# A two-block transformer kernel on one core: 176 stores of what GpSimd has written change from SyncE's queue to GpSimd's

## The chip, the cores and the metric

The kernel runs on one core of a Trainium2 chip. The metric is the time of one execution on the device, in microseconds (us), measured three times for the kernel before. Engine names are those of the profile: PE (TensorE), DVE (VectorE), ACT (ScalarE), POOL (GpSimd), SP (SyncE, which here only issues DMAs). PEclk is the clock that TensorE was granted, as a share of full speed.

## What is computed

A sequence of 2048 tokens of width 1024 goes through two blocks in float32. The first block (window attention, an HGRN2 branch, a mixture of experts) is not touched and is left out here. The second block, cut to what matters:

```python
xn = rms_norm(h, norm_gain)
qa, ka, va, ga, qb, kb, vb, gb, iq, ik, iw, za, zb = split(xn @ w_in)
ya = chunked_relpos_attention(qa, ka, va, rel_bias) * silu(ga)
qb, kb = partial_rope(qb, 16), partial_rope(kb, 16)
iq, ik = partial_rope(iq, 8), partial_rope(ik, 8)
yb = dsa_sparse_attention(qb, kb, vb, iq, ik, iw) * silu(gb)
merged = sigmoid(za + b0) * (ya @ w_branch_a) + sigmoid(zb + b1) * (yb @ w_branch_b)
h = rms_norm(h + merged @ w_out, final_norm_gain)
```

Both attentions have 8 heads of 64. The chunked one sees a band of 9 chunks of 64 keys; the sparse one picks up to 256 keys for each query by the score that iq, ik and iw give.

## The kernel before, in words

**Who sets the order.** The kernel carries a planner of its own. Each piece of work is a generator (a lane) that yields until the planner's clock says that its operands and its engine are free (`b.on(engine, tiles)`), and then emits its instruction. The order in which the generators are let through is the order of the instructions on each engine, and every engine, SP's DMA queue among them, works through its own in that order. `Engine.__getattr__` (from L100) wraps every call, so nearly all instructions have line L111; `Engine.cost` (from L123) gives the planner each call's cost. A `dma_start` there costs its bytes on a shared DMA time and nearly nothing on the issuing engine; an `indirect_dma_start` (GpSimd's gathers) costs 1.04 on GpSimd.

**The second block** is class S3 (from L1846). Its run (L2784) goes through stages, in the profile at about these times:

- to 2026 us: the norm (`norm_lane`), into which the end of the first block is woven (the combine step gathers two expert rows per token block with GpSimd's indirect DMAs, tiles `cy`, and adds them to `cx`), and the projections of the first half of the sequence that are needed by rows: `rows` (16 token blocks in all, 8 per half) makes a 128x256 piece of the projection on PE, `ev_n` (L2047) evicts it through ACT into a ring of three `st` tiles, has GpSimd rotate it in place (`rotate`, six small operations on `rot` and `st`), and stores it to DRAM through `store` (L2037): `IQ` (g = 1, one per token block) and `QB` (g = 2 and 3, two per token block), 128 KB each.
- 2026 to 2337 us: `chunked(0)`, the chunked attention of the first half in 32 units, with other projections on PE between them (the fill). `a_loads` (L2174) loads for every two units `K` (two DMAs), `Q` (four) and `V`, two buffers each, and for every eight units the bias `rb` (one buffer). `a_unit` makes scores on PE (`pS<-K,Q`), adds the bias and takes the maximum on DVE, exponentials on ACT; GpSimd normalises (`sc<-sc,ast`), PE transposes (`pT<-ident,sc`), ACT and DVE split the result into two parts (`pp`), and PE multiplies by V (`pU<-pp,V`). GpSimd copies part of the result (`ot<-up`), and `gate` (L2339) multiplies `ot` by the gate `sg` on GpSimd and stores it to `YT`, 64 KB, through `store`. `gate_load` (L2333) loads `sg` into two buffers.
- 2337 to 2985 us: the rest of the fill, then `sparse` over blocks 0 to 9, with the second half's row projections as fill. It ends every unit with the same `gate`. The normalised input of the second half is loaded from `XND` into `xnh` and `xnl` at the start, and `IQ` and `QB` are read back in tiles `x`.
- 2985 to 3340 us: `chunked(1)`, as chunked(0), for the second half; then the rest of its fill to about 3404 us.
- to the end: `sparse` over blocks 10 to 15, with the output part `tail` as fill. It loads gated rows from `YT` into `yt` (eight loads, one per chunk of the sequence) and gate values from `TZ`, adds with GpSimd (`m<-tz`) and multiplies with the output weights.

**The stores in question.** `store` waits until the planner sees the tile ready for "sync", issues the DMA on SP, and marks the tile done. 16 `IQ`, 32 `QB` and 128 `YT` stores are executed. What SP has behind a store, loads of K, Q, V, weights (`whi`, `wlo`) and gates, comes after it in SP's order.

Of the kernel before, what the change touches and what calls it, by code (L numbers as in the profile page):

```python
# [10 lines left out]
F32 = mybir.dt.float32  # L11
# [81 lines left out]
class Engine:  # L93
# [11 lines left out]
    def __getattr__(self, f):  # L105
        real = getattr(self.eng, f)
        if not callable(real) or f in ("preload_act_table_set",):
            return real

        def call(*a, **k):  # L110
            r = real(*a, **k)  # L111
            out = k.get("out", a[0] if a else None)
            if is_ap(out):
                outs = [out] + [k[x] for x in ("accum_out",) if is_ap(k.get(x))]
                ins = [x for x in a[0 if "out" in k else 1:] if is_ap(x)]
                ins += [x for y, x in k.items() if y not in ("out", "accum_out") and is_ap(x)]
                ins += [x.ap for x in k.values() if hasattr(x, "ap") and not is_ap(x) and is_ap(x.ap)]
                cost, lat = self.cost(f, out, ins, k, [x for x in a + tuple(k.values()) if isinstance(x, AF)])
                self.clock.op(self.name, outs, ins, cost, lat, 1.46 if f == "indirect_dma_start" else 0.0)
            return r  # L120
        return call

    def cost(self, f, out, ins, k, fs):  # L123
        n = out.free_size()
        if f in ("dma_start", "indirect_dma_start"):
            b = out.size() * 4 if callable(out.size) else out.size * 4
            return (1.04, 0.0) if f != "dma_start" else (b / 3.6e5, 0.0)
        if self.name == "tensor":
            if f == "transpose":
                return 0.109, 0.1  # L130
            if ins[0].dtype == F32:
                return max(0.2, n * 0.0017), 0.1
            return max(0.107, n * 0.000423), 0.1
        ps = any(x.space == PSUM for x in ins) or out.space == PSUM
        m = max([n] + [x.free_size() for x in ins])
        if self.name == "vector":
            if f in ("tensor_scalar", "tensor_copy", "memset") and not ps and "accum_out" not in k:
                return 0.067 + n * 0.00055, 0.07
            if f == "reciprocal":
                return 0.06 + n * 0.0063, 0.07  # L140
            return 0.067 + (0.05 if "accum_out" in k else 0.0) + m * 0.00107, 0.07
        if self.name == "scalar":
            aps = is_ap(k.get("scale")) + is_ap(k.get("bias")) + ("accum_out" in k)
            return self.switch(next((x for x in fs if hasattr(x, "name")), None)) + (0.052 if ps else 0.1) + m * 0.00083 + 0.09 * aps, 0.1
        return 0.13 + n * (0.00088 if f == "tensor_scalar" else 0.00217), 0.1
# [50 lines left out]
class B:  # L196
# [101 lines left out]
    def store(self, dst, t, tile=None):  # L298

        yield from self.do("sync", "dma_start", dst, t)  # L300
        self.done(t if tile is None else tile)
# [1544 lines left out]
class S3:  # L1846
# [187 lines left out]
                yield from b.on("tensor")  # L2034
        b.spawn(self.ev_n(g, blk, ps))

    def store(self, dst, t, src=None, key=None):  # L2037

        b = self.b
        yield from b.on("sync", t)  # L2040
        self.nc.sync.dma_start(dst, t.bitcast(F32) if src is None else src)
        b.done(t)
        if key:
            self.flags.add(key)
        yield 1

    def ev_n(self, g, blk, ps):  # L2047
# [14 lines left out]
        elif g:  # L2062
            h = 8 if g == 1 else 4
            x = yield from self.stage([128, h, 256 // h])
            yield from b.on("scalar", ps, x)
            nc.scalar.activation(x, ps[:, 0:256].rearrange("p (h d) -> p h d", h=h), AF.Copy)
            b.done(ps)
            yield 1
            yield from b.on("gpsimd", x)
            if g == 1:  # L2070
                self.rotate(x, rp[:, 16:20], rp[:, 20:24], 8, 4)
                dst, key = self.IQ[r, :], ("iq", blk)
            else:
                self.rotate(x, rp[:, 0:8], rp[:, 8:16], 4, 8)
                dst, key = self.QB[r, (g - 2) * 256:(g - 2) * 256 + 256], ("qb", blk, g - 2)
            yield 1
            yield from self.store(dst, x, x.rearrange("p h d -> p (h d)"), key)
        else:
            x = yield from self.stage([128, 424])
            yield from b.on("scalar", ps, x)  # L2080
            nc.scalar.activation(x[:, 0:160], ps[:, 0:160], AF.Copy)
            nc.scalar.activation(self.iw[:, blk], ps[:, 160:168], AF.Copy, scale=1.0 / 16)
            b.done(ps)
            nc.scalar.activation(self.vbS[:, blk, 0], x[:, 64:128], AF.Copy)
            yield 1
            yield from b.on("vector", x)
            b.lo(self.vbS[:, blk, 1], x[:, 64:128], self.vbS[:, blk, 0])
            yield 1
            yield from b.on("gpsimd", x)
            self.rotate(x[:, 0:64].unsqueeze(1), rp[:, 0:8], rp[:, 8:16], 1, 8)  # L2090
            self.rotate(x[:, 128:160].unsqueeze(1), rp[:, 16:20], rp[:, 20:24], 1, 4)
            xx = x[:, 168:424].rearrange("p (i d) -> p i d", i=2)
            nc.gpsimd.tensor_copy(xx[:, 0].rearrange("p (a d) -> p a d", a=2), x[:, 0:64].unsqueeze(1).to_broadcast([128, 2, 64]))
            nc.gpsimd.tensor_copy(xx[:, 1].rearrange("p (a d) -> p a d", a=4), x[:, 128:160].unsqueeze(1).to_broadcast([128, 4, 32]))
            yield 1
            pt = yield from b.bank("pT")
            yield from b.on("tensor", xx, pt)
            for i in range(2):
                nc.tensor.transpose(pt[:, i * 128:i * 128 + 128], xx[:, i], b.ident)
            b.done(x)  # L2100
            yield 1
            kk, ii = self.kbS[:, r], self.ikS[:, r]
            yield from b.on("scalar", pt)
            nc.scalar.activation(kk, pt[:, 0:128], AF.Copy)
            nc.scalar.activation(ii, pt[:, 128:256], AF.Copy)
            yield 1
            yield from b.on("vector", kk)
            b.lo(kk[64:128], pt[64:128, 0:128], kk[64:128])
            b.lo(ii[32:64], pt[32:64, 128:256], ii[32:64])
            b.lo(ii[96:128], pt[96:128, 128:256], ii[96:128])  # L2110
            b.done(pt)
            self.flags.add(("kb", blk))
            yield 1
# [225 lines left out]
    def gate(self, ot, g, i, blk):  # L2339

        b = self.b
        yield from b.G("tensor_tensor", ot, ot, g, op=OP.mult)
        b.done(g)
        yield from self.store(self.YT[i, :, blk * 128:blk * 128 + 128], ot, None, ("y", i, blk))

    def a_units(self, half):
        for p in range(4):
# [690 lines left out]
```

## Time and profile before

| | |
|---|---|
| runs | 4229.81, 4234.5 and 4241.1 us, median 4234.5 |
| the profiled execution | 4238.96 us, of it 4237.1 us in the profile's span |
| PE busy | 3719.6 us, 88% of the span |
| DVE busy | 2733.3 us, 65% |
| ACT busy | 2263.5 us, 53% |
| POOL busy | 787.0 us, 19% |
| mean granted clock | 0.939 |

Matmuls overlap, so the busy time of PE is the time in which at least one is under way. A wait is put down to what came last by the profile; "SPq" is SP's DMA queue, and a wait of SPq means that its next DMA had not been issued yet. DMAs that SP issues are shown with the time that the issue took on SP.

### The profile page before, as it was taken

What the parts mean: (1) busy time and instruction counts of PE and PEld (TensorE: products, weight loads), DVE (VectorE), ACT (ScalarE), POOL (GpSimd) and SP (SyncE); (2) the same over time, 40 slices, a digit from 0 to 9 for tenths busy, and PEclk for the clock granted to TensorE, in tenths of its full rate; (3) what the DMA queues carried; (4) which work ended last, traced back from release to release, by engine and by line L of the source; (5) the groups of instructions that cost most, each with busy time, mean ns of one, the idle gap of its engine ahead of it and who ended that gap; (6) DMA issues with size and microseconds to landing.
All of it is one profiled execution on the core that took longest, in us unless ns stands there. A gap on an engine that the chain in (4) does not pass through costs nothing. (4 is left out here: it accounts for less than half of the span.)

```text
span 4237.1 us, 64813 instructions
## 1 busy us (share of the span) xinstructions
PE 3719.6 (88%) x21649; PEld 3211.7 (76%) x21649; DVE 2733.3 (65%) x7027; ACT 2263.5 (53%) x4628; POOL 787.0 (19%) x1474
## 2 busy tenths in 40 slices
PE   3999999979889995779888899998788979998895
PEld 2888788768768884778777798886677868997685
DVE  7866875787777776562445256777544248878772
ACT  3644645556456664342334167886444238876851
POOL 1310000131011112650334242000222101111000
PEclk9999999979999997899989989999899999999898
DMA  6232542144288886588888834432666488886154
GB/s 221 80 130 73 183 141 90 34 144 140 105 303 316 310 312 248 196 314 275 272 240 265 293 111 133 142 111 63 177 176 189 135 270 299 298 282 222 48 183 172
DMA packets 451953, 815.32 MB, mean 192 GB/s; under 512 B 129712, under 2 KB 269968, under 8 KB 450704
## 3 DMA queue, kind: packets, MB, share of 16 engines
q1 hardware_dynamic: 440080, 777.42, 55.2%
q0 software_dynamic: 11520, 33.57, 2.5%
q8 instruction: 176, 2.88, 0.3%
q14 instruction: 177, 1.45, 0.1%
HBM read 589.56 MB, written 229.65 MB: 193 GB/s over the span
## 5 line engine op out<-in xcount | busy, mean ns | idle before, releaser
L111 PE MATMUL pA<-xnl,whi 128*128 128x512 f32 x1024 | 417.8, 408 | 2.9 <-POOL whi L111 2.9
L111 DVE TENSOR_TENSOR wlo<-ld,whi 128x1024 fp32r<-128x1024 f32 x271 | 325.1, 1230 | 140.4 <-POOL whi L111 74.0
L111 ACT ACTIVATE pp<-pT 128x256 fp32r<-128x256 f32 (+1 forms) x568 | 260.8, 478 | 283.7 <-PE pT L111 277.4
L111 PE MATMUL pA<-xnh,wlo 128*128 128x512 f32 x1024 | 407.1, 398 | 2.3 <-DVE wlo L111 2.3
L111 PE MATMUL pA<-xnh,whi 128*128 128x512 f32 x1024 | 407.5, 398 | 0.0
L111 DVE TENSOR_TENSOR pp<-pT,pp 128x256 fp32r<-128x256 f32 (+1 forms) x568 | 295.9, 539 | 138.7 <-ACT pp L111 135.6
L111 PE MATMUL pA<-hlo,whi 128*128 128x512 f32 x832 | 352.8, 424 | 10.0 <-issue 6.6
L111 PE MATMUL pA<-hhi,wlo 128*128 128x512 f32 x832 | 329.7, 396 | 0.0
L111 PE MATMUL pA<-hhi,whi 128*128 128x512 f32 x832 | 328.9, 395 | 0.0
L111 PE MATMUL pU<-pp,vbS 128*128 128x256 f32 x1088 | 217.2, 311 | 34.5 <-DVE pp L111 23.3
L111 ACT ACTIVATE whi<-ld 128x1024 fp32r<-128x1024 f32 x212 | 213.3, 1052 | 50.7 <-PE pA L111 35.0
L111 DVE SCALAR_TENSOR_TENSOR acc<-rl,iw,acc 128x512 f32<-128x512 f32 (+3 forms) x304 | 212.7, 700 | 36.2 <-ACT rl L111 26.4
L111 PEld LDWEIGHTS pA<-xnh,wlo 128*128 128x128 f32 x1024 | 196.3, 192 | 47.3 <-DVE wlo L111 3.4
L111 PE MATMUL pA<-wlo,xnh 128*128 128x256 f32 (+1 forms) x672 | 205.0, 305 | 24.4 <-ACT st L111 5.9
L111 ACT ACTIVATE bias<-acc,sst 128x384 f32<-128x384 f32 (+13 forms) x168 | 219.9, 1309 | 8.6 <-DVE sst L111 6.1
L111 PEld LDWEIGHTS pA<-xnl,whi 128*128 128x128 f32 x1024 | 197.3, 193 | 33.6 <-POOL whi L111 3.3
L111 PEld LDWEIGHTS pA<-xnh,whi 128*128 128x128 f32 x1024 | 197.3, 193 | 30.2
L111 PEld LDWEIGHTS pU<-pp,vbS 128*128 128x128 f32 x1088 | 164.0, 198 | 53.6 <-DVE pp L111 33.5
L111 PE MATMUL pA<-whi,xnl 128*128 128x256 f32 (+1 forms) x672 | 200.0, 298 | 4.1 <-DMA xnl<-XND 4.1
L111 PE MATMUL pA<-whi,xnh 128*128 128x256 f32 (+1 forms) x672 | 199.8, 297 | 0.0
L111 PE MATMUL pS<-kbS,qd 128*128 128x512 f32 (+3 forms) x640 | 186.4, 391 | 13.5 <-DVE bst L111 9.6
L111 PE MATMUL pS<-K,Q 128*128 128x320 f32 (+3 forms) x480 | 117.7, 354 | 79.8 <-DMA Q<-QA 75.7
(491 smaller groups left out, 10993.7 us busy)
## 6 DMA issues: line engine op xcount, KB each, us to landing
whi<-W2P SPq DMA_DIRECT2D x172, 512.0 KB
wlo<-W2P SPq DMA_DIRECT2D x172, 512.0 KB
ld<-in_w_gu_dram SPq DMA_DIRECT2D x128, 512.0 KB
ld<-in_w_dn_dram SPq DMA_DIRECT2D x64, 512.0 KB
W2P<-whi SPq DMA_DIRECT2D x57, 512.0 KB
W2P<-wlo SPq DMA_DIRECT2D x57, 512.0 KB
Y<-ym SPq DMA_DIRECT2D x48, 512.0 KB
K<-KA SPq DMA_DIRECT2D x48, 384.0 KB
```

Source lines behind the costliest of these rows:

```text
L111: r = real(*a, **k)
```

## The change

`store` gets an argument for the engine that issues the DMA. The rotated queries (`IQ`, `QB`) and the gated rows (`YT`) are issued on GpSimd's queue, all other stores stay on SP's. The planner prices a plain DMA of an engine other than SP as it prices a gather: 1.04 on the engine, and its bytes on the DMA time.

```diff
-                self.clock.op(self.name, outs, ins, cost, lat, 1.46 if f == "indirect_dma_start" else 0.0)
+                far = 1.46 if f == "indirect_dma_start" else out.size() * 4 / 3.6e5 if f == "dma_start" and self.name != "sync" else 0.0
+                self.clock.op(self.name, outs, ins, cost, lat, far)
...
-            return (1.04, 0.0) if f != "dma_start" else (b / 3.6e5, 0.0)
+            return (1.04, 0.0) if f != "dma_start" or self.name != "sync" else (b / 3.6e5, 0.0)
...
-    def store(self, dst, t, src=None, key=None):
+    def store(self, dst, t, src=None, key=None, eng="sync"):
 
         b = self.b
-        yield from b.on("sync", t)
-        self.nc.sync.dma_start(dst, t.bitcast(F32) if src is None else src)
+        yield from b.on(eng, t)
+        getattr(self.nc, eng).dma_start(dst, t.bitcast(F32) if src is None else src)
...
-            yield from self.store(dst, x, x.rearrange("p h d -> p (h d)"), key)
+            yield from self.store(dst, x, x.rearrange("p h d -> p (h d)"), key, "gpsimd")
...
-        yield from self.store(self.YT[i, :, blk * 128:blk * 128 + 128], ot, None, ("y", i, blk))
+        yield from self.store(self.YT[i, :, blk * 128:blk * 128 + 128], ot, None, ("y", i, blk), "gpsimd")
```

On SP, at the end of sparse blocks 0 to 9 and the start of chunked(1) (numbers behind the names are buffers), the order before:

```order
L111 DMA YT<-ot_32974 128x128
L111 DMA sg_33060<-SG 128x128
L111 DMA YT<-ot_33081 128x128
L111 DMA sg_33155<-SG 128x128
L111 DMA YT<-ot_33173 128x128
L111 DMA YT<-ot_33230 128x128
L111 DMA rb_33241<-in_relb_dram 128x2x640
L111 DMA K_33243<-KA 64x2x768
L111 DMA Q_33245<-QA 64x2x256 x2
```

and now:

```order
L111 DMA sg_32953<-SG 128x128
L111 DMA sg_33060<-SG 128x128
L111 DMA sg_33155<-SG 128x128
L111 DMA rb_33241<-in_relb_dram 128x2x640
L111 DMA K_33243<-KA 64x2x768
L111 DMA Q_33245<-QA 64x2x256 x2
```

The first loads of chunked(1) follow the last gate load; the four stores of gated rows no longer stand among them. PE's order at this place is the same in both.

On POOL, in chunked(1), before (three units' gates and the normalisations around them):

```order
L111 TENSOR_TENSOR ot_34513<-up_34471 64x128 x2
L111 TENSOR_TENSOR ot_34513<-ot_34513,sg_34535 128x128
L111 TENSOR_SCALAR sc_34459<-sc_34459,ast 128x640
L111 TENSOR_SCALAR sc_34495<-sc_34495,ast 128x640
L111 TENSOR_SCALAR sc_34545<-sc_34545,ast 128x640
L111 TENSOR_TENSOR ot_34614<-up_34585 64x128 x2
```

and now, at about the same place:

```order
L111 TENSOR_TENSOR ot_34571<-up_34538 64x128 x2
L111 TENSOR_SCALAR sc_34522<-sc_34522,ast 128x640
L111 TENSOR_TENSOR ot_34571<-ot_34571,sg_34581 128x128
L111 DMA YT<-ot_34571 128x128
L111 TENSOR_SCALAR sc_34531<-sc_34531,ast 128x640
L111 TENSOR_TENSOR ot_34676<-up_34642 64x128 x2
```

The store stands behind its gate product, and a normalisation for which PE's transposes wait can stand right behind the store.

On POOL, in the row projections of the first half, before (one QB row, one key row, one IQ row):

```order
L111 TENSOR_TENSOR rot<-st_19477,rope 128x32 x4
L111 TENSOR_TENSOR st_19477<-rot 128x4x8 x2
L111 TENSOR_TENSOR cx_19332<-cx_19332,cy_1_19251 128x1024
L111 TENSOR_TENSOR rot<-st_19520,rope 128x8 x4
```

and now:

```order
L111 TENSOR_TENSOR rot<-st_19477,rope 128x32 x4
L111 TENSOR_TENSOR st_19477<-rot 128x4x8 x2
L111 TENSOR_TENSOR cx_19332<-cx_19332,cy_1_19251 128x1024
L111 DMA QB<-st_19477 128x256
L111 TENSOR_TENSOR rot<-st_19520,rope 128x8 x4
```

Each of the 24 rotated rows of this half is followed by its store on POOL. Further on, the gathers of the combine step for token blocks 8 to 15, which stood among these rows before, now come behind all of them.

## Rows read from the trace of the kernel before

**Rows 1.** The page: busy us, share of the span, instructions of each engine.

```profile
PE 3719.6 (88%) x21649; PEld 3211.7 (76%) x21649; DVE 2733.3 (65%) x7027; ACT 2263.5 (53%) x4628; POOL 787.0 (19%) x1474
```

**Rows 2.** Busy time by stage: us, PE, PEld, DVE, ACT, POOL, PEclk, DMA share, GB/s.

```profile
1790.00:1900.00 110.00, 83.18 (x632) 80.98 (x631) 64.26 (x125) 48.78 (x94) 60.66 (x98) 0.92 0.91 319
...
2026.00:2337.00 311.00, 275.51 (x1401) 232.43 (x1400) 162.38 (x512) 116.58 (x287) 123.94 (x179) 0.93 0.85 259
...
2985.00:3340.00 355.00, 301.99 (x1578) 259.67 (x1579) 167.39 (x587) 146.09 (x349) 96.47 (x169) 0.89 0.67 183
```

**Rows 3.** PE's waits in chunked(1), 2985 to 3340: us, times, longest.

```profile
PE pS L111 <- DMA Q<-QA: 49.1, 20, 12.3
```

**Rows 4.** PE's waits in chunked(0), 2026 to 2337.

```profile
PE pS L111 <- DMA Q<-QA: 24.7, 14, 5.6
```

**Rows 5.** Waits of SP's queue in chunked(1), 2985 to 3340.

```profile
SPq L111 <- POOL ot L111: 111.6, 24, 10.7
```

**Rows 6.** Waits of SP's queue in chunked(0), 2026 to 2337.

```profile
SPq L111 <- POOL ot L111: 32.9, 14, 4.3
```

**Rows 7.** SP at the start of chunked(1): start, us, operation, count.

```profile
2973.42 0.38 SPq L111 DMA_DIRECT2D sg<-SG  x1
2979.08 8.17 SPq L111 DMA_DIRECT2D YT<-ot  x2
...
2990.36 1.25 SPq L111 DMA_DIRECT2D Q<-QA  x2
```

**Rows 8.** POOL before that: the last gate products of the sparse blocks.

```profile
2978.60 0.46 POOL L111 TENSOR_TENSOR ot<-ot,sg 128x128 f32<-128x128 f32 x1 [5.38 <-DVE sg L111]
...
2986.45 0.46 POOL L111 TENSOR_TENSOR ot<-ot,sg 128x128 f32<-128x128 f32 x1 [7.16 <-DVE sg L111]
```

**Rows 9.** PE in chunked(1); in brackets the idle time before, and its releaser.

```profile
2997.31 1.81 PE L111 MATMUL pS<-K,Q 128*128 128x320 f32 x4 [12.35 <-DMA Q<-QA]
...
3008.53 0.61 PE L111 MATMUL pS<-K,Q 128*128 128x320 f32 x1 [1.75 <-DMA Q<-QA]
...
3129.24 1.28 PE L111 MATMUL pS<-K,Q 128*128 128x320 f32 x4 [1.64 <-DMA K<-KA]
...
3304.32 1.81 PE L111 MATMUL pS<-K,Q 128*128 128x320 f32 x4 [3.36 <-DMA Q<-QA]
```

**Rows 10.** SP in chunked(1), around one pair of stores.

```profile
3110.59 0.32 SPq L111 DMA_DIRECT2D sg<-SG  x1
3116.20 2.22 SPq L111 DMA_DIRECT2D YT<-ot  x2
```

**Rows 11.** PE and SP where the second half's input is loaded.

```profile
2424.25 0.48 PE L111 MATMUL pA<-wlo,xnh 128*128 128x168 f32 x1 [5.60 <-DMA xnh<-XND]
...
2410.05 4.11 SPq L111 DMA_DIRECT2D x<-IQ  x4
```

**Rows 12.** DMAs by tile: duration of the issue, least/median/most ns.

```profile
L111 POOL DMA_INDIRECT cy<-Y,pos x32: 987/1007/1971, 1651.4 to 1870.5; - x32
...
L111 SPq DMA_DIRECT2D YT<-ot x128: 319/320/1483, 2074.3 to 4149.2; - x128
```

**Rows 13.** POOL in the row projections: one rotated row, and a gather behind another.

```profile
1765.47 0.89 POOL L111 TENSOR_TENSOR rot<-st,rope 128x32 f32<-128x32 f32 x4 [1.77 <-ACT st L111]
1766.43 0.46 POOL L111 TENSOR_TENSOR st<-rot 128x32 f32<-128x32 f32 x2
...
1792.03 0.99 POOL L111 DMA_INDIRECT cy<-Y,pos  x1 [0.30 <-issue]
```

**Rows 14.** A normalisation on POOL and PE's transposes behind it, chunked(0).

```profile
2154.08 1.59 POOL L111 TENSOR_SCALAR sc<-sc,ast 128x640 f32<-128x640 f32 x2
...
2155.94 0.60 PE L111 MATMUL pT<-ident,sc 128*128 128x128 f32 x4
```

**Rows 15.** The chain that ends last, near the last load of gated rows.

```profile
4149.18 1.61 DMA YT<-ot
...
4150.93 5.25 DMA yt<-YT
```

## The prediction

> **What bounds the kernel now.** I read the page first: PE is busy for 3719.6 us, POOL for 787.0 [rows 1]. PE is the bound, so a change pays only where PE stands idle or runs at a low clock. Then I cut the second block into stages [rows 2]. The reader is to see two things: PE is busy for 302 of 355 us in chunked(1) and for 276 of 311 in chunked(0), so 53 and 35 us are idle there; and the DMA share is 0.67 in the one, 0.85 in the other, so the transfers alone would fill the time in neither. Next come the waits of PE in these stages: nearly all of the idle time ends with a load of Q, 49.1 us in chunked(1) [rows 3] and 24.7 us in chunked(0) [rows 4]. Last the waits of SP, which issues those loads: in chunked(1) it stands 111.6 us on GpSimd's gate product `ot` [rows 5], in chunked(0) 32.9 us [rows 6]. Only the store of that product can hold SP on it, and the loads stand behind the store. So part of PE's waits for Q is a queue held up by stores. What is to be found is how large a part.
>
> **The change part by part.**
>
> *The start of chunked(1).* SP issues the last gate load at 2973.42 and is then held by two stores until 2987.25; rb, K and Q follow, the last pair of Q at 2990.36 [rows 7]. The product that frees the last store ends at 2986.91 [rows 8]. PE waits 12.35 us and starts the scores at 2997.31 [rows 9], 5.7 us after the end of the last Q issue. In the new order the loads follow that gate load at about 2973.8, 13.5 us sooner, if nothing else holds them. The buffers of one half of the loads may be freed only with the product that ends at 2979.06 [rows 8]; then K and two Q, 1.9 us of issue [rows 7], K taken like one Q, end at 2981, and with the same 5.7 us the scores start at 2986.7, about 10.6 us sooner. Bounds 10.6 and 12.35; I take **-11**, the near one.
>
> *The rest of chunked(1).* Later in the stage SP is idle from 3110.91 until a pair of stores at 3116.20 [rows 10], and K goes out behind them at 3118.4; without the stores it can go up to 7.5 us sooner. PE's wait for that K, 1.64 us, would go. I matched loads and gaps over the stage: four gaps are behind loads that a store held by more than the gap, or nearly, the first 1.64 and the last 3.36 us, 9.85 in all [rows 9]; with the 1.75 us of the second unit [rows 9] that is 11.6. The other gaps stand behind loads that wait for a buffer, a weight load or a gate store ahead on SP, and I leave them. Late next is such a load, so I take three quarters: **-9**, bounds 0 and -36.7 (all waits for Q but the first).
>
> *chunked(0).* By the same share, 11.6 of 36.7, 7.8 of the 24.7 us would go. But SP is held by the product for 32.9 us here and for 111.6 there [rows 5, 6], and DMA is busier [rows 2]. I take about half, **-4**; bounds 0 and -24.7.
>
> *The load of the second half's input.* PE waits 5.60 us for `xnh`, whose load SP issues behind four loads of IQ that take it 4.11 us [rows 11]. In the new order those loads of IQ stand behind `xnh` and `xnl`. **-4**; bounds 0 and -5.6.
>
> *SP's own issue time.* 176 stores of 0.32 us [rows 12] are 56 us less on SP. They lie beside PE; where PE waits for SP they are in the terms above. **0**.
>
> *GpSimd's new work.* Before shows no plain store by GpSimd. The nearest row is its gather: 1.0 us in the median, 1.97 at most [rows 12], with 0.3 us ahead of the next [rows 13]; I take 1.3 us. From below it may cost what SP pays, 0.32 us; from above 2.3. 176 stores are 229 us more on an engine that is idle for four fifths of the time [rows 1]. That is hidden except where PE waits for GpSimd next. Such a place is a normalisation: one ends at 2155.67 and PE's transposes start 0.27 us later [rows 14]. By the same matching, about 25 of the 128 normalisations of the two stages have under 1 us to spare. With a store ahead of half of them, at some 0.6 us past the slack, that is **+7**; bounds 0 and, with one store ahead of a normalisation in each of 64 units and no cover at all, 64 x 1.3 = +83.
>
> *The row projections.* POOL rotates a row in 1.4 us (0.89 + 0.46) [rows 13] and now adds 1.3. If all 24 rows of the first half showed this, it would be +31. The stage at 1790 to 1900 has 27 us of idle PE and 49 of idle POOL [rows 2], and SP no longer waits for rotated rows ahead of its weight loads, which could give back up to those 27. The gathers of the combine come later on POOL, so some transposes move behind projections. I see no sign that prevails: **0**, bounds -27 and +31, in which about 10 either way is what I count with.
>
> *The last gated rows.* At the end the store lands 1.61 us after its product, and the load behind it takes 5.25 [rows 15]. GpSimd's store takes some 0.7 to 1.5 us longer to issue. That is on the path here and perhaps at one other of the eight loads of `yt`: **+2**, bounds 0 and 8 x 1.5 = +12.
>
> *The clock.* The clock granted is 0.89 in chunked(1) and 0.93 in chunked(0), where PE has gaps [rows 2]. If 24 us fewer of gaps raise it by a hundredth in both, 302 + 276 us shrink by some 6; I take half, **-3**, bounds -9 and 0.
>
> Sum: -11 -9 -4 -4 +7 +2 -3 = **-22 us**. The profiled execution took 4238.96 us and would take 4217; it lies 4.5 us above the median of the three runs, so against the median I say 4212.5, rounded to **4212 us**.
>
> *A rule that speaks against this.* SP is held for 13.4 us by stores that need 0.3 us each [rows 7, 12]: the loss is waiting in order, not issuing. The Trainium skill (DMA: Bandwidth & Descriptors, section "Issuing engines are not separate DMA queues") says that starting DMAs from several engines only saves the time of initiating them, usually small beside the DMA. By that rule the gain would be the issue time of SP, which is hidden, and the result the first rival below. The trace does not contradict that transfers share the 16 DMA engines; it shows a cost that the rule does not count.
>
> **The rivals.**
>
> *Nothing to measure.* Behind the stores stand other things that hold the same loads: two buffers of K and Q, weight loads that wait for PE, gate stores. For it: of the 36.7 us of waits for Q behind the first, 25.1 stand behind loads that the matching does not put down to a store. Against it: the first gap is behind stores alone. Then only -11 -4 are won and +7 +2 lost: -6, about **4228 us**.
>
> *Slower: GpSimd becomes the wait.* If a store by GpSimd takes 2.3 us there, and stands ahead of a normalisation that PE needs, the wait moves from SP to POOL. For it: the gather's price at its largest [rows 12], and the normalisation without slack [rows 14]. Against it: POOL is busy for only 96 of 355 us in chunked(1) [rows 2]. With 32 of the 64 stores of these stages ahead of a normalisation and 1.3 us of each past the slack, +42 in place of +7: 4212 + 35 = **4247 us**. It decides from where a store of the 64 shows more than 29/64 = 0.45 us on average (7 + 22 = 29).
>
> The same page (section "SWDGE vs HWDGE vs iDMA") says that GpSimd's DMAs have their descriptors written by software on that engine, and that SP's are made in hardware with a faster setup. No row here shows a plain store on both; by it the price lies above SP's 0.32 us, as the gather's row has it.
>
> *A larger gain.* If SP, free of the stores, runs ahead with all loads, half of what is left of the waits for Q (73.8 - 24 = 50) goes too: 4212 - 25 = **4187 us**. Against it: the DMA share of 0.85 in chunked(0), and two buffers.
>
> *The order itself.* The planner now sees costs on POOL and orders differently on all engines. That can move the row projections by the 10 us either way named above; it is in the range.
>
> **How the numbers follow.** A measurement of this kernel tells about 0.3%, 12.7 us, from no change. The forecast has a chance of 0.5, the larger gain 0.14, nothing to measure 0.18, slower by GpSimd 0.18. The forecast's own spread (about 10 us by the row projections) puts some of it above 4221.8, and some of the rival without effect below it: faster 0.62, same 0.22, slower by over 0.3% (above 4247.2) 0.16: most of the slower rival, whose price lies just at that line, with its worse bounds behind it. The range takes in the larger gain and the slower rival's price, from 4182 to 4248; beyond them stay the bounds of +83 and the -36.7, about 1 in 5 together.
>
> **What would show it.** Right: SP's waits on POOL's `ot` are gone in both chunked stages; rb, K and Q of the first unit of chunked(1) go out at about 2974 to 2981 in this time scale, and the gap of 12.35 falls below 3; the waits for Q fall from 49.1 to about 28 and from 24.7 to about 20; a store on POOL shows 1.0 us. Wrong: waits of PE for `sc` (or its weights from POOL) over 20 us; a store of 2 us; the first gap as it was, with the loads held by something else; or a stage before 2026 longer by more than 10 us.

## The result, and the profile after

The changed kernel takes 4183.5 us in the median (4174.66 to 4198.95, four runs), the kernel before beside it 4237.67 (4229.81 to 4241.1). The ratio is 0.9879, with a 95% interval of 0.9844 to 0.9913: about 51 us faster, where 22 were forecast. It lies inside the range given (4182 to 4248), at its lower edge; two of the four runs lie below that range.

The page of the changed kernel, busy time by engine, against [rows 1]:

```profile
PE 3700.0 (88%) x21649; PEld 3197.9 (76%) x21649; DVE 2731.1 (65%) x7027; ACT 2266.8 (54%) x4628; POOL 873.2 (21%) x1650
```

POOL has 176 instructions and 86 us more. PE runs the same 21649 matmuls in 20 us less of busy time, though no matmul was taken away.

**Where the time went.** Both kernels execute 21649 matmuls in nearly the same order, so the start of the n-th matmul is a clock of progress. The table gives how much earlier (-) or later (+) than in the kernel before a stage is passed through, from the traces of single profiled executions. "Old order" and "new order on SP" are the first two experiments below.

| stage (time before, us) | forecast | changed kernel | old order | new order on SP |
|---|---|---|---|---|
| up to 1706 (program unchanged) | 0 | -6.8 | -4.3 | -0.4 |
| row projections, to 2028 | 0 | +8.0 | +6.8 | +4.2 |
| chunked(0) and fill, to 2349 | -4 | -10.7 | -5.1 | -8.9 |
| second half's input, to 2475 | -4 | +6.4 | -0.2 | +9.9 |
| sparse blocks 0 to 9, to 2975 | | +11.7 | +3.9 | +10.1 |
| start of chunked(1), to 2997 | -11 | -12.5 | -12.5 | -0.1 |
| chunked(1) and its fill, to 3379 | -9 | -44.4 | -22.4 | -27.0 |
| the rest | +2 | -1.5 | 0.0 | +0.7 |
| sum | | -49.8 | -33.8 | -11.5 |

The forecast has two further terms that belong to no one stage: +7 for GpSimd's work and -3 for the clock. The first line shows what two executions of the same instructions differ by, so a difference of a few us in any one line says little. Chunked(1) with its start gains 56.9 us, more than the whole; the other stages lose 7.1 on balance.

**The start of chunked(1).** SP in the changed kernel, against [rows 7]:

```profile
2972.27 9.71 SPq L111 DMA_DIRECT2D sg<-SG  x2
2982.09 0.38 SPq L111 DMA_DIRECT2D rb<-in_relb_dram  x1
2982.58 0.58 SPq L111 DMA_DIRECT2D K<-KA  x1
```

PE at the same place, against the first of [rows 9]:

```profile
2993.12 0.48 PE L111 MATMUL pU<-pp,vbS 128*128 128x256 f32 x2
2993.44 0.76 PE L111 MATMUL pS<-K,Q 128*128 128x320 f32 x4
2997.46 4.71 PE L111 MATMUL pS<-K,Q 128*128 128x320 f32 x12 [3.27 <-DVE ast L111]
```

The loads follow the last gate load at once. They go out 10.5 us before the last products of the sparse blocks are multiplied (`pU`), and PE passes from one stage to the next without a gap: the 12.35 us are gone. Late next is the maximum on DVE, 3.27 us. SP is not free of GpSimd's products ahead of these loads: its gate loads, which stand directly behind each other now, wait there for a buffer of `sg` that a product frees, and the last of them sets when `rb`, K and Q go out. SP's waits on `ot` from 2972 us to the end of the stage:

```profile
SPq L111 <- POOL ot L111: 26.6, 3, 17.2
```

**The rest of chunked(1).** PE's waits there, changed kernel, against [rows 3]:

```profile
PE pS L111 <- DMA Q<-QA: 7.0, 8, 2.6
PE pS L111 <- DVE ast L111: 3.9, 2, 3.3
PE pT L111 <- POOL sc L111: 2.4, 4, 1.1
```

Waits for Q fell from 49.1 to 7.0 us, and the gate products, which held SP for 111.6 us [rows 5], are no longer among what SP waits for within the stage; in their place stand the weight loads, which wait for PE:

```profile
SPq L111 <- PE pA L111: 89.3, 16, 10.5
SPq L111 <- DVE ast L111: 28.0, 4, 10.9
SPq L111 <- ACT st L111: 24.7, 10, 5.6
```

The next four rows are from the view by windows and set the same work side by side: the 1750 matmuls from the first score of chunked(1) on. Columns as in [rows 2]. The kernel before:

```profile
2997.30:3378.60 381.30, 340.58 (x1748) 291.64 (x1749) 166.54 (x584) 150.54 (x355) 95.62 (x166) 0.91 0.64 180
```

the changed kernel:

```profile
2993.40:3330.30 336.90, 321.32 (x1750) 276.84 (x1749) 167.52 (x587) 150.84 (x356) 115.57 (x202) 0.97 0.72 203
```

Of the 44.4 us, 25.1 are idle time of PE (40.7 before, 15.6 after) and 19.3 are busy time: the same matmuls took 340.6 and then 321.3 us, and the granted clock rose from 0.91 to 0.97. A single gap of the kernel before shows how:

```profile
3179.20 1.49 PE L111 MATMUL pS<-K,Q 128*128 128x320 f32 x4 [3.55 <-DMA Q<-QA]
```

The windows are 10 us ahead of this gap of 3.55 us, the 5.3 us behind it, and the next 5.4:

```profile
3165.00:3175.00 10.00, 10.00 (x62) 8.96 (x61) 6.07 (x21) 6.22 (x16) 5.44 (x9) 1.00 0.46 110
3179.20:3184.50 5.30, 5.30 (x19) 4.95 (x20) 1.60 (x7) 1.56 (x4) 0.46 (x1) 0.50 1.05 376
3184.60:3190.00 5.40, 5.40 (x33) 4.77 (x33) 4.19 (x18) 2.79 (x8) 1.65 (x3) 1.00 0.01 3
```

PE works through all three, but in the second at a granted clock of 0.50, the lower of its two levels (1.2 GHz), with 19 matmuls where the next stretch of about the same length has 33. The gap cost 3.55 us and then half of 5.3, about 2.6 more. The Trainium skill (TensorE: Matmul & The Clock Gate, section "Part 1: The HAM clock gate") tells of the same two levels, with the lower one behind idling; the trace agrees, 0.50 here.

The longest stretch at 0.50 (first row) is the one behind the first gap of the kernel before, of 12.35 us; in the changed kernel (second row) it is the one behind the wait of 3.27 us for DVE:

```profile
2997.31:3017.31 20.00, 15.76 (x48) 11.08 (x49) 8.74 (x37) 7.33 (x18) 3.98 (x5) 0.50 1.03 324
2997.50:3007.70 10.20, 8.80 (x27) 6.34 (x28) 6.61 (x29) 4.76 (x11) 3.14 (x4) 0.50 1.02 262
```

Not every gap is followed by one. Of the twelve gaps of over 1 us that lie behind that stretch in the kernel before, nine are followed by 3.4 to 6.6 us of work at 0.50; three, of 1.29, 1.30 and 1.79 us, by none. In all PE works 56.5 us of these 1750 matmuls at 0.50 in the kernel before and 18.7 in the changed kernel. Half of the difference is 18.9 us, nearly all of the 19.3.

**What got worse.** At the load of the second half's input PE waits, in the changed kernel, for a weight:

```profile
2409.31 0.33 PE L111 MATMUL pT<-ident,x 128*128 128x128 f32 x1 [0.66 <-DMA x<-QB]
2431.99 0.48 PE L111 MATMUL pA<-wlo,xnh 128*128 128x168 f32 x1 [22.35 <-DMA wlo<-W2P]
```

and SP had issued four tiles of 2 MB ahead of that weight:

```profile
2407.05 0.42 SPq L111 DMA_DIRECT2D xnh<-XND  x1
2407.52 0.43 SPq L111 DMA_DIRECT2D xnl<-XND  x1
2407.99 0.44 SPq L111 DMA_DIRECT2D whi<-W2P  x1
2408.60 0.60 SPq L111 DMA_DIRECT2D xnh<-XND  x1
2409.24 0.50 SPq L111 DMA_DIRECT2D xnl<-XND  x1
2409.79 0.46 SPq L111 DMA_DIRECT2D wlo<-W2P  x1
```

Before, PE waited here for `x`, `xnh` and `xnl` in turn, 3.19, 5.60 and 4.05 us, 12.8 in all.

**The price of a store by GpSimd.** From the view by tile, against [rows 12]:

```profile
L111 POOL DMA_DIRECT2D YT<-ot x128: 537/582/628, 2078.6 to 4101.1; - x128
```

0.58 us, and 0.28 to 0.29 between the product and it: not the gather's 1.0 which the forecast took. At the end of the chain the store lands 1.92 us after it begins where SP's landed after 1.61 [rows 15].

### The profile page after: what moved, and what is told of

Same layout as the page of the kernel before. It is cut to its first block, busy times and chain, and to the rows that moved or that the text cites. A ratio compares the mean times of both kernels' runs of the same rounds, so it can differ in the third digit from the quotient of the medians.

```text
span 4185.7 us, 64744 instructions
## 1 busy us (share of the span) xinstructions
PE 3700.0 (88%) x21649; PEld 3197.9 (76%) x21649; DVE 2731.1 (65%) x7027; ACT 2266.8 (54%) x4628; POOL 873.2 (21%) x1650
## 5 line engine op out<-in xcount | busy, mean ns | idle before, releaser
L111 ACT ACTIVATE bias<-acc,sst 128x384 f32<-128x384 f32 (+13 forms) x168 | 220.2, 1310 | 17.2 <-DVE sst L111 14.5
L111 ACT ACTIVATE rl<-pS 128x512 f32<-128x512 f32 (+3 forms) x304 | 159.6, 541 | 51.4 <-PE pS L111 28.0
```

## The experiments

Ratios are to runs of the kernel before on the same chip, with 95% intervals. The theories that the expectations name: A, SP stood in order on GpSimd's products, and PE's loads stood behind; B, the planner's new order brings the gain; C, the rotated rows' move gains too; D, GpSimd's own queue or SP's saved issue time; S, GpSimd becomes the wait; E and F, two views of what the new order does in chunked(1); G, two buffers of `ot` were the limit.

### Old order, stores on GpSimd

```diff
-                self.clock.op(self.name, outs, ins, cost, lat, 1.46 if f == "indirect_dma_start" else 0.0)
+                self.clock.op("sync" if f == "dma_start" else self.name, outs, ins, cost, lat, 1.46 if f == "indirect_dma_start" else 0.0)
...
-        self.nc.sync.dma_start(dst, t.bitcast(F32) if src is None else src)
+        getattr(self.nc, eng).dma_start(dst, t.bitcast(F32) if src is None else src)
```

> All 176 stores go to GpSimd's queue, but the planner prices and orders everything as in the kernel before: every other instruction on every engine keeps its place. Theory A (the queue: SP was held in order by stores that waited for GpSimd's product, and PE's loads stood behind them): chunked(1) gains by itself about as much as the change did there, PE's waits for Q there fall from 49.1 to under 15 us and the whole is 40 to 65 us faster than before, more than the change, since the new wait of 22 us at the load of the second half's input (new order) is not there. Theory B (the new order of the planner brings the gain, the queue does not): within 13 us of before, waits for Q in chunked(1) over 35 us.

Measured: 4212.65 us, ratio 0.9956 (0.9939 to 0.9973), 19 us faster. The profiled execution took 4203.57 us, the shortest of its four; its stages in the table sum to 33.8 us where the medians differ by 22, so they show where the time went and not its size to better than some 10 us. PE's waits in chunked(1):

```profile
PE pS L111 <- DMA Q<-QA: 26.1, 11, 5.2
PE pS L111 <- DVE ast L111: 3.3, 1, 3.3
```

and the same 1750 matmuls:

```profile
2985.90:3344.80 358.90, 326.32 (x1750) 281.17 (x1749) 167.32 (x587) 151.05 (x356) 115.17 (x202) 0.95 0.67 190
```

A is right in its mechanism and wrong in its size: the first gap goes as in the changed kernel (-12.5) and 22.4 us behind it, 8.1 of idle time and 14.3 of clock. The waits for Q stay at 26.1, over the 15 that A allowed; SP now stands on weight loads and gate stores:

```profile
SPq L111 <- PE pA L111: 92.2, 17, 14.8
SPq L111 <- ACT st L111: 61.3, 9, 11.2
```

B's "within 13 us" does not hold either. The wait of 22 us is not there, as expected.

### New order, stores on SP

```diff
+        if eng == "gpsimd":
+            s = t.bitcast(F32) if src is None else src
+            self.nc.sync.eng.dma_start(dst, s)
+            self.nc.gpsimd.clock.op("gpsimd", [dst], [s], 1.04, 0.0, dst.size() * 4 / 3.6e5)
+        else:
+            getattr(self.nc, eng).dma_start(dst, t.bitcast(F32) if src is None else src)
```

> The order of the changed kernel on all engines, but the 176 stores are issued by SP, at the place where the planner lets them through. Theory A (queue): SP waits for GpSimd's product again (over 80 us in chunked(1)), PE's waits for Q there come back to 35 us or more, and the whole is as slow as before or up to 25 us slower, 4230 to 4260 us, with the order's own losses (the wait for wlo of some 22 us near 2430). Theory B (order): near the changed kernel, under 4200 us.

Measured: 4227.14 us, ratio 0.9972 (0.9954 to 0.9989), between what A and B expected. PE in chunked(1):

```profile
PE pS L111 <- DMA Q<-QA: 32.4, 17, 12.2
PE pS L111 <- DMA K<-KA: 3.1, 2, 2.0
```

SP at the same time (the store's line is that of this kernel's edit):

```profile
SPq L2044 <- POOL ot L111: 121.3, 26, 7.5
SPq L111 <- PE pA L111: 39.6, 12, 7.3
```

The hold is back, with its first gap of 12.2 us, and so is the wait for `wlo` (23.3 us). Still chunked(1) is 27 us shorter than before. The order alone does something there, which A had not expected. Counted in the order of PE's instructions, the chunked(1) of the new order has 678 projection matmuls between its first and its last score; the order before has 612. The 66 more can run while loads land; that they do is argued from the count, not shown. The two experiments with before and the changed kernel make a square; the entries are the gaps ahead of scores in chunked(1), us:

| | 612 between the scores | 678 |
|---|---|---|
| stores on SP | 51.0 | 36.5 |
| stores on GpSimd | 30.6 | 12.9 |

Each of the two takes 14.5 to 23.6 us off, whatever the other does. Of what the stores' move takes off, 12.3 are the first gap. Behind it the move takes off 8.1 us in the old order and 11.3 in the new one, and the new order 14.5 and 17.7: there the order does more than the queue.

The same square for the whole time, by the ratios: the stores' move alone (the old order) brings 19 us, the new order alone 12, both together 51 (37 to 66). With every other instruction in its place the move is thus worth 19 us in the old order and 39 in the new one, and a good part of the 51 needs both.

### Gated rows only

```diff
-            yield from self.store(dst, x, x.rearrange("p h d -> p (h d)"), key, "gpsimd")
+            yield from self.store(dst, x, x.rearrange("p h d -> p (h d)"), key)
```

> Only the 128 stores of gated rows (YT) go to GpSimd, priced as in the change; the rotated rows stay on SP. Theory A: the gain of chunked(1) stays (start of its units about 50 us or more sooner against before, waits for Q under 15 us), and what the change lost before 2040 us in the row projections (some 14 us) is not lost: 10 to 20 us faster than the changed kernel, 4163 to 4175 us. Theory C (rotated rows on SP hold SP as well, and their move gains too): slower than the changed kernel by 5 us or more.

Measured: 4195.31 us, ratio 0.9903 (0.9885 to 0.9921): most of the gain (0.9879) is here, but not the 10 to 20 us more that A expected; by the medians it is slower than the changed kernel, as C has it, though the intervals overlap. The order is another too, so this run does not tell what moving the rotated rows' stores brings by itself: chunked(1) has 639 matmuls between its scores and 32.3 us of gaps, waits for Q 27.9.

### Rotated rows only

```diff
-        yield from self.store(self.YT[i, :, blk * 128:blk * 128 + 128], ot, None, ("y", i, blk), "gpsimd")
+        yield from self.store(self.YT[i, :, blk * 128:blk * 128 + 128], ot, None, ("y", i, blk))
```

> Only the 48 stores of rotated rows (IQ, QB) go to GpSimd; gated rows stay on SP. Theory A: chunked(1) is as before (waits for Q about 49 us), and the row projections lose some 10 to 15 us by the gathers that come later: 4235 to 4255 us. Theory C: faster than before by 5 us or more in the stage 1650 to 2040.

Measured: 4209.41 us, ratio 0.9939 (0.9922 to 0.9956), a miss for A: 26 us faster. The stage in which these stores are made does lose, 9.7 us from 1706 to 2028, so C's reason is not it. By the trace the time is won later: 18.7 us in the sparse blocks 0 to 9 and 11 in the last part, where no rotated row is stored but the order differs. The waits for Q in chunked(1) stay at 44.2. Why this order suits the sparse blocks was not looked into.

### Each store one gate later, still on SP

```diff
+        if late:
+            s = t.bitcast(F32)
+            self.nc.sync.clock.op("sync", [dst], [s], dst.size() * 4 / 3.6e5)
+            self.flush()
+            self.late = (dst, s, t.tensor.name)
+        else:
+            self.nc.sync.dma_start(dst, t.bitcast(F32) if src is None else src)
...
```

`flush` issues the store that was put off; it is called by the next gate, and when the buffer is to be used again.

> The kernel before, with all stores on SP and every other instruction in its old place, but each store of gated rows of the chunked stages and of sparse blocks 0 to 9 is issued one gate later on SP, when its product is long done (the last two before the first loads of chunked(1) stay where they were). Theory A (what cost time was SP standing in order on a product, not issuing, and not the queue that moves the bytes): in chunked(1) behind the first gap as much is gained as by the move to GpSimd with the old order, 15 to 22 us; the first gap stays at about 12; the whole is 12 to 25 us faster than before. Theory D (GpSimd's own queue or SP's saved issue time brings it): within 6 us of before.

Measured: 4250.14 us, ratio 1.0041 (1.0025 to 1.0058), slower. GpSimd's waits say why:

```profile
POOL ot L111 <- DMA YT<-ot: 100.3, 18, 11.6
```

It was 16.8 us before. There are two buffers of `ot`, and a late store keeps one of them; GpSimd waited for it, and PE for GpSimd (15.4 us for `sc` in chunked(0)). This run does not tell A from D, and was made again with four buffers, below.

### A dearer store

```diff
         b.done(g)
+        self.nc.gpsimd.eng.tensor_tensor(self.toll, self.toll, self.toll, op=OP.mult)
+        self.nc.gpsimd.eng.tensor_tensor(self.toll, self.toll, self.toll, op=OP.mult)
```

> The changed kernel with two needless operations of 128x256 (0.9 us each) on GpSimd between each product and its store of gated rows, which the planner does not count: a store then costs GpSimd some 2.4 us in place of 0.6, about the upper price of the prediction. Theory A (GpSimd has room): 5 to 30 us over the changed kernel, still faster than before. Theory S (GpSimd becomes the wait that ends last): PE's waits for the normalisation over 40 us and 50 us or more over the changed kernel, slower than before.

Measured: 4209.41 us, ratio 0.9953 (0.9939 to 0.9968); the changed kernel has 0.9879, so the toll cost about 31 us (26 in the profile, 5.5 of it ahead of 1706, where no toll is paid). The two operations took less than the 0.9 us each that were expected, about 0.61:

```profile
L2345 POOL TENSOR_TENSOR toll<-toll x128: 603/613/2162, 2084.3 to 4124.6; 128x256 f32<-128x256 f32 x128
```

From the end of a product to the end of its store GpSimd takes 1.79 us in the median, where the changed kernel takes 0.88: twice as much, not four times. The toll is spread over the second block; PE's waits for the normalisation from 2000 us on are

```profile
PE pT L111 <- POOL sc L111: 16.9, 14, 2.5
```

against 10.4 in the changed kernel. S is out at this price: 157 us of work more on GpSimd (1029.9 busy, after 873.2) showed as 26 to 31, and the kernel is still faster than before. The 2.3 us of the prediction's slower rival were not reached.

### Another price in the planner

```diff
-            return (1.04, 0.0) if f != "dma_start" or self.name != "sync" else (b / 3.6e5, 0.0)
+            return (1.04 if f != "dma_start" else 0.6, 0.0) if f != "dma_start" or self.name != "sync" else (b / 3.6e5, 0.0)
```

> The changed kernel with a plain DMA of GpSimd priced at 0.6 in the planner in place of 1.04 (0.58 us is what the trace shows). Only the order changes: 627 projection matmuls lie between the score groups of chunked(1), where the changed kernel has 678 and the kernel before 612. Theory E (the planner, once the stores are off SP, gives a good order there whatever the exact price): within 8 us of the changed kernel. Theory F (how many projection matmuls happen to lie between the groups decides how much of the loads is covered): gaps of chunked(1) 20 us or more (13 in the changed kernel), 8 to 20 us slower than the changed kernel in that stage.

Measured: 4172.33 us, ratio 0.9866 (0.9846 to 0.9886). In chunked(1) it comes as F has it: 28.5 us of gaps, and from the first score on the stage gains 23.0 us on the kernel before where the changed kernel gains 44.4, 21 us less. But E's statement on the whole is right too, for another reason: the sparse blocks 0 to 9, which had lost 11.7 us, won 9.0. So the size of the order's part in any one stage is not fixed by the change.

### The second pair of the input later

```diff
-                    fill = chain(self.proj(0, range(8, 32), last=True), self.xn_load(2), self.xn_load(3), self.proj(1, range(12), groups=True))
+                    fill = chain(self.proj(0, range(8, 32), last=True), self.xn_load(2), self.xn_late(3), self.proj(1, range(12), groups=True))
```

`xn_late` starts a lane that waits 4 us on the planner's clock and then does `xn_load`.

> The changed kernel, but the load of the second pair of xnh and xnl (4 MB) is held back by 4 us of the planner's time, so that the weights of the row projections go ahead of it. If the new wait of 22 us at wlo comes from the 8 MB ahead of it on SP, it falls to 10 to 15 us and the stage 2337 to 2475 gains about 8. The order of chunked(1) changes as well (624 projection matmuls between the groups): by theory F that stage gives 8 to 20 us back, by theory E it does not.

Measured: 4178.6 us, ratio 0.9881 (0.9864 to 0.9898). PE's wait at this place:

```profile
PE pA L111 <- DMA wlo<-W2P: 13.9, 2, 13.5
```

The longest fell from 22.4 to 13.5, as expected if the bytes ahead on SP were its cause. The stage 2349 to 2475 did not gain the 8 us expected of it: it is 6.5 us behind the kernel before, as the changed kernel is (6.4), and the stage ahead of it gained 6.3 more; the order differs there too. Chunked(1), with 624 matmuls between its scores, has 28.6 us of gaps, as F has it; the whole is no faster by the interval.

### Four buffers of the product, and late stores with them

```diff
-        ot = yield from P.get([128, 128], F32, "ot", bufs=2)
+        ot = yield from P.get([128, 128], F32, "ot", bufs=4)
```

The first run has this edit alone, in both attentions; the second adds the late stores on SP. PE and GpSimd have the same order in the two.

> The kernel before with four buffers for the product ot in place of two, nothing else edited; the planner then orders the second block a little otherwise. Theory A (SP is held by the product's own time, not by its buffers): waits of SP on POOL ot in chunked(1) stay over 80 us, PE's gaps there over 40 us, and the whole lies within 20 us of before: that is what a new order alone can do. Theory G (the two buffers were the limit): the gaps of chunked(1) fall under 30 us.

> The same with each store of gated rows one gate later on SP (chunked stages and sparse blocks 0 to 9); order on PE and GpSimd as in the run with four buffers. With four buffers GpSimd no longer waits 100 us for late stores to land, as it did with two. Theory A (standing in order on the product is the cost, whichever queue moves the bytes): 12 to 25 us faster than the run with four buffers, gaps of chunked(1) behind the first 9 us or more smaller. Theory D (GpSimd's queue or SP's issue time): within 6 us of it.

Measured: 4233.22 us with four buffers, ratio 1.0003 (0.9987 to 1.0019), and 4212.44 us with late stores, ratio 0.9940 (0.9918 to 0.9963). Waits of PE, and of SP's queue, in chunked(1), four buffers:

```profile
PE pS L111 <- DMA Q<-QA: 50.9, 21, 12.3
```

```profile
SPq L111 <- POOL ot L111: 111.9, 26, 9.5
```

and with late stores:

```profile
PE pS L111 <- DMA Q<-QA: 40.4, 16, 12.4
```

```profile
SPq L2051 <- POOL ot L111: 35.4, 8, 8.0
```

G is out: more buffers alone change nothing. GpSimd no longer waits for a store to land. A is borne out: with every store still on SP, the late ones at 0.42 us of issue in the median (0.32 before), and every byte through the same queue, putting a store behind what need not wait for its product is worth 21 us. The gaps behind the first fell by 6 us, not by the 9 expected, with 35.4 us of SP's standing on products left. In the profile chunked(1) has 7.5 of 18.4 us; 4.6 lie ahead of 1706, where nothing was changed, and the rest is spread.

The run with four buffers also tells what a new order alone does. Stage by stage it is 8.5 us slower than before in chunked(0), 15.6 faster in the sparse blocks and 5.8 slower in the last part, and 2.8 faster in all.

### Two versions that go on from there

The first has the price of 0.6 and the late second pair together; the second adds this:

```diff
-            yield from self.store(self.TZ[i, :, s], t, None, ("tz", i, c))
+            yield from self.store(self.TZ[i, :, s], t, None, ("tz", i, c), "scalar")
```

> The changed kernel with both edits that were faster in the profile: price 0.6, and the second pair of xnh and xnl held back by 4 us of the planner's time. If both gains add, the wait at the second half's input falls from 15 to about 8 and the whole is 5 to 10 us faster than either, some 4160 to 4170 us; if the order scatters more than that, 4165 to 4190.

> The run before with one edit more by the same principle: the 64 stores of TZ, which ACT has just written, are issued by ACT's queue. SP's waits on ACT st in chunked(1) (67.7 us with price 0.6) fall below 35. If these hold the loads that PE waits for, the gaps of chunked(1) fall from some 28 to under 20 and the whole gains 5 to 15 us; if the weight loads that wait for PE hold them anyway, or ACT's 64 issues show, nothing is gained.

Measured: 4163.87 us, ratio 0.9823 (0.9800 to 0.9847), and 4154.77 us, ratio 0.9798 (0.9769 to 0.9826). The input's wait in the first did not fall to 8 (10.2 for `xnh` and 4.2 for `xnl`), so its lower time is not explained by that edit. In the second SP no longer stands on what ACT has written; it stands on the weight loads all the longer, 131.7 us in place of 98.1 in the first:

```profile
SPq L111 <- PE pA L111: 131.7, 18, 13.6
SPq L111 <- DVE ast L111: 27.5, 5, 12.9
SPq L111 <- DMA TZ<-st: 19.2, 7, 5.1
```

The waits for Q in chunked(1) fell from 25.1 to 19.3 us, the gaps from 31.0 to 25.3 rather than under 20. The planner's order differs between the two as well, so the second edit's own part is not shown. By the intervals the two cannot be told apart; both beat the changed kernel's ratio, the last one clearly.

## Why the prediction was right, and where its sizes were wrong

The direction and the mechanism held: SP stood in order on stores that waited for GpSimd, PE's loads stood behind them. Moving the stores with every other instruction in its place is worth 19 us in the old order and 39 in the new one, and the late stores show that the standing costs some 21 us by itself, with all issuing and all bytes still on SP. That the issue time saved on SP adds nothing, as the prediction has it, is not shown: the late stores gain 7.5 us in chunked(1), the stores on GpSimd in the old order 34.9 with its start.

That the time lies in the range is luck in part. What carried it to the edge is the clock and the planner's order, for which the sum had -3 and 0; the input's step, wrong in its sign, took 10 us back.

The rule that was weighed (the Trainium skill, DMA: Bandwidth & Descriptors, section "Issuing engines are not separate DMA queues") counts the issue time alone. It leaves out what counted here: the old order with GpSimd's stores is 19 us faster. No run here contradicts what it says of the shared DMA engines.

Point by point, in the prediction's own steps:

- **The start of chunked(1)**, -11: measured -12.5, in the change and with the old order alike, 0 where the stores stayed on SP. Right.
- **The rest of chunked(1)**, -9: measured -44.4. The matching of loads and gaps was good for what it counted: with the old order the idle time behind the first score fell by 8.1 us. Waits for Q are 7.0 us, not the 28 of the sign given. Two things were not in it. One is the **clock**, the step that gave -3 by a hundredth of clock for all gaps together, without a reason for the hundredth: it gave 14.3 us with the old order, and 19.3 in the changed kernel, as PE's work at 0.50 fell from 56.5 to 29.5 and 18.7 us. [rows 2] would have told more: an estimate in proportion, 0.11 of clock missing with 53 us of gaps, gives some 0.04 for 20 us less, about 13 us. The other is the order: the gaps "behind loads that wait for a buffer, a weight load or a gate store" were left as they were, but in the new order, which has 66 more projection matmuls between the scores, most of them went too, 17 us of idle time more (32.6 with the old order, 15.6 in the changed kernel).
- **chunked(0)**, -4: measured -10.7, of which the old order alone shows -5.1. For the queue the size is near: with the old order the waits for Q fell by 3.0 us, from 24.7 to 21.7; with the new one they are 13.1, where the sign said 20. The rest is order and clock. (The 24.7 are 70% of the idle time of this stage, not nearly all.)
- **The load of the second half's input**, -4: measured +6.4. This step failed in its sign. It looked at which load was ahead of `xnh` and not at what stood ahead of the weight that the same matmul needs: 8 MB, the second 4 of which nobody needed yet. Holding those back took 9 us off the wait, though not off the stage.
- **GpSimd's new work**, +7: PE's waits for `sc` in the two chunked stages rose from 1.4 to 10.3 us, and to 8.6 with the old order, so the term was near. In part that is luck: a store took 0.88 us with the time ahead of it and not 1.3, and with the old order seven more normalisations showed, not twelve, for some 1.0 us each and not 0.6. With 0.9 us more per store the kernel lost 26 to 31 us.
- **The row projections**, 0 with 10 either way: +8.0, +6.8 with the old order. Inside the bound. Kernels in which neither the stores nor the order of this stage changed show +1.4 to +6, so little more can be said.
- **The last gated rows**, +2: about 0.6 by the rows, hidden in -1.5.
- **The order itself**, put at 10 us for the row projections alone: it moved every stage of the second block, +9.9 at the input, +10.1 in the sparse blocks, -27.0 in chunked(1) with the stores on SP. This was the largest omission. The matmuls between the scores can be counted in the program's order ahead of a run; that their number gives the size is not shown (below).

Of the rivals, the larger gain (4187 us) came nearest. That more than half of the remaining waits for Q go as well is what happened in chunked(1), but not by its mechanism, an SP free of the stores that runs ahead: with the old order SP is as free, and 26.1 us of waits stay. The slower rival did not decide: a store took 0.58 us, and at 1.79 with the toll the kernel lost 26 to 31 us, not enough to lose what the queue gives.

What stays open: why the sparse blocks gain up to 24 or lose up to 12 us by the order; and whether the order's 27 us in chunked(1) come from the planner having SP free or by chance. The other versions whose planner has SP free of the gated rows have only 618 to 639 matmuls there, which speaks for chance. How the matmuls cover the loads is open too: with these stores on GpSimd the gaps ahead of the scores are 30.6 us at 612 matmuls, 25.3 at 618, 28.6 at 624, 28.5 and 31.0 at 627, 32.3 at 639 and 12.9 at 678, so among the first six the number decides nothing, and where the matmuls lie was not looked into.

## What to carry to other kernels

A store waits for its producer, and on a queue that works in order every load behind it waits too; look for a wait of the DMA queue on a slow producer just ahead of loads that the bounding engine waits for, and either give the store to the engine that made the data or put it behind the loads (with more buffers: with two of them the late stores made the kernel slower, with four faster). Count a gap on TensorE at its length plus what the clock takes behind it: here 25.1 us of gaps less gave 19.3 us of busy time back as well. Where a planner sets the order, a small edit moves every stage, here by up to 16 us in a run whose sum did not move, so a forecast has to give the order a range of its own, and a mechanism is to be tested with the order held fixed.

## What the hardware showed that was not expected

- After 3.55 us without a matmul the granted clock was 0.50 for 5.3 us, then 1.00 again, with PE at work throughout; in 1750 equal matmuls busy time fell by 19.3 of the 44.4 us, with 37.8 us less of work at 0.50. Of twelve later gaps of over 1 us nine were followed by work at 0.50, three were not.
- A plain store takes GpSimd 0.58 us (0.54 to 0.63 over 128 of them; 0.58 as well for the 48 of 128 KB), as against 1.0 for a gather, and ACT 0.33 (64 stores of `TZ`).
- A store put off on SP is not free: with two buffers it made GpSimd wait 100.3 us for landings instead of 16.8, and the kernel slower than before.
